# Input projections of a hybrid decoder block on one Trainium2 core: direct products, and seven products of quarters (Strassen) in two halves of the tokens

## Chip, cores and metric

The kernel runs on one core of one Trainium2 chip. The metric is the device time of one execution in microseconds (us). The kernel before was timed in three runs; the figure that stands for it is their median. The span of the profile is a profiled execution of its own.

## The reference

One decoder block over 2048 tokens of width 1024. The change lies in the first product, `xn @ w_in`, whose 6152 columns are q, k and v (1024 each), 8 forget logits, an attention gate, the input of a linear recurrent unit and its gate (1024 each):

```python
def rmsnorm(x, g):
    y = xf * lax.rsqrt(jnp.mean(xf * xf, axis=-1, keepdims=True) + RMS_EPS) * g
...
xn = rmsnorm(h, pre_gain[i])
z = xn @ w_in[i]
q, k, v, fl, g_attn, x_lru, g_lru = jnp.split(z, SPLIT_POINTS, axis=-1)
fl = fl + b_f[i]
o_attn = forgetting_attention(q, k, v, fl)          # 8 heads of 128, causal, scale 128 ** -0.5
y_attn = rmsnorm(o_attn, attn_out_gain[i]) * jax.nn.silu(g_attn)
xc = causal_depthwise_conv(x_lru, conv_w[i], conv_b[i])       # 4 taps
o_lru = rg_lru(xc, ...)       # two 128x128 gates per block of channels, then a scan over the tokens
y_lru = rmsnorm(o_lru, lru_out_gain[i]) * jax.nn.silu(g_lru)
mix = jnp.concatenate([y_attn, y_lru], axis=-1) @ w_out[i]
...
```

After it come a norm, the per-layer input embeddings and a sigmoid gate of another 1024x1024 product. All values are float32.

## The kernel before

**Products in three parts.** A float32 operand is split into a high part in TensorE's reduced format (fp32r) and a low part: `split` (L44) lets ScalarE round the high part (L46) and VectorE or GpSimd subtract it from the source (L52). `mm3` (L55) multiplies high by high, high by low and low by high (L60 to L62), so a product of two operands takes three matmuls, all added up in PSUM.

**Operands.** The tokens come transposed from memory (`xT`), the columns of a chunk being 512 tokens. Four chunks of x times the gain of the norm are split into `xh` and `xl` (L224 to L234), 8 pieces of 128 channels in each; they stay in SBUF to the end of the projections. The scale of each token's norm is computed beside it: ScalarE squares rows of x (L243), `rsqrt_small` takes the root, and a product with a diagonal matrix spreads the scales over the partitions (`rx`, L253). It is applied only when a result leaves PSUM.

**Value projection.** `load_wv` loads and splits weights of two heads (256 columns, 264 with the forget logits), `project_v` (L188) multiplies them with 16 blocks of 128 tokens as the stationary operand. The first two of the four groups are mixed with the loading of the chunks.

**The other projections** run over the eight head blocks `hb`. For each, `load_w` (L309) loads and splits 128 columns of weights, and `project` (L319) makes one bank of PSUM for a chunk: 8 pieces times 3 matmuls of 512 columns. In this order: x_lru for all chunks (L357 to L370), the convolution on VectorE (L367), the gate g_lru (L376 to L382), k, and between k's chunks the two gates of the recurrent unit (12 matmuls for each 512 tokens) with their chain: sigmoids, tanh and square root on ScalarE, reciprocal, two products, a scan and the gated output on VectorE (L401 to L413), the product with XC, the square and the sum of squares on GpSimd (L405, L420, L421). Then q and the attention gate of the head block before (L427). `spill` (L324) scales the result and stores it to memory. GpSimd also makes the low parts of most weights and of XC.

**What sets the order.** Each engine works off its own queue in the order in which a planner lays the program; tiles of the pools (`bank` 6, `wf` 2, `wh` 2 and so on) tie the queues to one another. All loads and stores of this stage are issued by SyncE (SP), in order. Attention (all of head 0's keys and values are loaded and split during the last projections, `load_part`, L432), the output product and the last gate follow; the change leaves their code, apart from the engine that splits keys and values (GpSimd becomes VectorE) and the place of the query's scale.

Of the kernel before, what the change touches and what calls it, by code (L numbers as in the profile page):

```python
# [65 lines left out]
def hymba_kernel(ctx: ExitStack, tc: tile.TileContext, x, xT, pT, w_t, w_v3, w_v4, w_o, w_ple, w_pg,  # L66
# [96 lines left out]
    def load_wv(pool, j):  # L163

        n = 264 if j == 3 else 256
        src = w_v4 if j == 3 else w_v3[j]
        wh = pool.tile([P, KD, 264], F32R, name="wvh")
        wl = pool.tile([P, KD, 264], F32R, name="wvl")
        yield wh, wl
        for q in range(4):  # L170
# [4 lines left out]
            yield

    def all_wv(pool, j):
        steps = load_wv(pool, j)
        w = next(steps)
        for _ in steps:  # L180
            pass
        return w

    def project_v(w, j, t2s=range(8)):
        n = 264 if j == 3 else 256
        wh, wl = w
        for t2 in t2s:
            vo = pva.tile([P, 2, 256], F32, name="vo", bufs=2)  # L188
            for ti in range(2):
                tb = t2 * 2 + ti  # L190
                ts = slice(tb % 4 * P, (tb % 4 + 1) * P)
                b = bank()
                for k in range(KD):
                    mm3(nc, b[:, :n], (xh[tb // 4][:, k, ts], xl[tb // 4][:, k, ts]), (wh[:, k, :n], wl[:, k, :n]),
                        k == 0, k == KD - 1)
                nc.scalar.activation(vo[:, ti], b[:, :256], AF.Copy, scale=rs_x[:, tb:tb + 1])
                if j == 3:
                    nc.vector.tensor_scalar(zf[:, :, tb], b[:, 256:264], rs_x[:, tb:tb + 1], None, ALU.mult)
# [4 lines left out]
    with ExitStack() as pv:  # L203
# [919 lines left out]
```

## Time and profile before

| | us |
|---|---|
| median of 3 runs | 2305.82 |
| lowest, highest run | 2304.03, 2310.03 |
| span of the profiled execution | 2304.8 |
| first matmul | 5.7 |
| end of the projections | 1139 |

| stage (profiled execution) | us |
|---|---|
| value projection and loading of x | 0 to 200 |
| the eight head blocks and the last two weights | 200 to 1139 |
| attention, output product, last gate | 1139 to 2304.8 |

How to read it: the page gives each engine's busy time, its share of the span and its instructions. PE is TensorE's matmuls, PEld its weight loads (beside the matmuls), DVE is VectorE, ACT ScalarE, POOL GpSimd, SP SyncE. A row of a group names the line, the engine, the operation, output and input tiles with their shapes, the count, then the busy time, the mean duration in ns, and the idle time of the engine ahead of the group with what ended it. A row of the timeline has the start, the duration, the engine, the line and the tiles. Matmuls overlap one another, so the duration of one is longer than the distance of two.

### The profile page before, as it was taken

The numbers are of one execution on the slowest core, as the hardware profiler recorded it, in microseconds if no ns is written. First come the engines' busy times: TensorE is split into PE (matmuls) and PEld (weight loads), VectorE is DVE, ScalarE is ACT, GpSimd is POOL, SyncE is SP. The second block draws the span as 40 slices with busy tenths as digits, with TensorE's granted clock in tenths as the row PEclk, the third lists the DMA queues.
The fourth block names the chain that finished last, engine by engine and source line by source line (L and its number), as shares of the span: only waits on it lengthen the run. The fifth ranks groups of instructions, "written<-read, shape, count | busy, mean of one in ns | idle before, by whom it ended". The sixth has DMA issues, their size and how long they took to land.

```text
span 2304.8 us, 30692 instructions
## 1 busy us (share of the span) xinstructions
PE 2271.1 (99%) x11425; PEld 1888.1 (82%) x11425; DVE 1205.8 (52%) x2190; ACT 929.2 (40%) x1558; POOL 668.5 (29%) x597
## 2 busy tenths in 40 slices
PE   8999999999999999999999999999999999999999
PEld 8998888888888888888788888888878887888887
DVE  5222675454546454546388888888833213333333
ACT  7312433332323232323267677776744323221111
POOL 0130323232323232313123344333544223222221
PEclk9999999999999999999999999999999999999999
DMA  9411112121212120212445444444446436333332
GB/s 339 138 51 37 53 48 78 37 85 37 85 37 85 37 85 32 81 35 79 130 124 158 147 157 144 134 123 139 157 123 203 153 126 201 131 104 119 107 108 75
DMA packets 169014, 249.02 MB, mean 108 GB/s; under 512 B 14241, under 2 KB 87201, under 8 KB 168865
## 3 DMA queue, kind: packets, MB, share of 16 engines
q1 hardware_dynamic: 168720, 247.03, 33.8%
q8 instruction: 89, 1.46, 0.3%
q14 instruction: 61, 0.49, 0.1%
q10 hardware_dynamic: 144, 0.05, 0.0%
HBM read 171.26 MB, written 75.76 MB: 107 GB/s over the span
## 4 chain that ended last, share of the span: by engine, by line
PE 93%; ACT 2%; DVE 2%; DMA 2%; issue 1%; SPq 0%; POOL 0%; ACTq 0%; DVEq 0%
PE bank L60 24%; PE bank L62 24%; PE bank L61 24%; PE tbank L665 5%; PE sbank L60 3%; PE obank L61 2%; PE obank L62 2%; PE sbank L61 2%; PE sbank L62 2%; PE obank L60 2%; ACT pr L638 1%; DMA kvf<-kT_d 1%; PE ebank L60 1%; PE ebank L61 1%; PE ebank L62 1%; PE tbank L684 1%
## 5 line engine op out<-in xcount | busy, mean ns | idle before, releaser
L60 PE MATMUL bank<-xh,wh 128*128 128x512 f32 x1280 | 506.0, 395 | 0.0
L61 PE MATMUL bank<-xl,wh 128*128 128x512 f32 x1280 | 505.9, 395 | 0.0
L62 PE MATMUL bank<-xh,wl 128*128 128x512 f32 x1280 | 505.9, 395 | 0.0
L61 PEld LDWEIGHTS bank<-xl,wh 128*128 128x128 f32 x1280 | 240.5, 188 | 58.0
L62 PEld LDWEIGHTS bank<-xh,wl 128*128 128x128 f32 x1280 | 240.5, 188 | 58.0
L60 PEld LDWEIGHTS bank<-xh,wh 128*128 128x128 f32 x1280 | 240.5, 188 | 57.8
L52 DVE TENSOR_TENSOR tl<-tbank,th 128x512 fp32r<-128x512 f32 (+1 forms) x320 | 192.8, 608 | 86.1 <-ACT th L46 82.2
L46 ACT ACTIVATE th<-tbank 128x512 fp32r<-128x512 f32 (+1 forms) x320 | 169.4, 532 | 132.4 <-PE tbank L665 129.7
L52 POOL TENSOR_TENSOR wl<-wf,wh 128x512 fp32r<-128x512 f32 x70 | 96.1, 1394 | 265.0 <-ACT wh L46 265.0
L665 PE MATMUL tbank<-ident,pr 128*128 128x128 f32 x1088 | 172.2, 274 | 0.0
L638 ACT ACTIVATE pr<-pr,m 128x128 f32<-128x128 f32 (+15 forms) x128 | 154.3, 1205 | 40.1 <-DVE m L629 38.9
L665 PEld LDWEIGHTS tbank<-ident,pr 128*128 128x128 f32 x1088 | 134.4, 141 | 29.2 <-issue 0.2
L60 PE MATMUL sbank<-kh,qh 128*128 128x512 f32 (+3 forms) x320 | 137.6, 430 | 15.2 <-DVE m L629 13.0
L60 PE MATMUL bank<-wvh,xh 128*128 128x256 f32 (+1 forms) x512 | 144.0, 285 | 7.2 <-ACT wvh L46 7.2
L52 POOL TENSOR_TENSOR yo<-yf,yh 128x1024 fp32r<-128x1024 f32 x32 | 76.9, 2403 | 255.8 <-ACT yh L46 255.7
L62 PE MATMUL bank<-wvh,xl 128*128 128x256 f32 (+1 forms) x512 | 144.5, 284 | 0.0
L61 PE MATMUL bank<-wvl,xh 128*128 128x256 f32 (+1 forms) x512 | 144.1, 283 | 0.0
L60 PE MATMUL obank<-th,vh 128*128 128x512 f32 (+1 forms) x320 | 123.7, 387 | 0.8 <-ACT th L46 0.8
L61 PE MATMUL obank<-tl,vh 128*128 128x512 f32 (+1 forms) x320 | 118.4, 370 | 1.2 <-DVE tl L52 0.6
L61 PE MATMUL sbank<-kl,qh 128*128 128x512 f32 (+3 forms) x320 | 117.5, 367 | 0.0
L62 PE MATMUL obank<-th,vl 128*128 128x512 f32 (+1 forms) x320 | 117.4, 367 | 0.0
L62 PE MATMUL sbank<-kh,ql 128*128 128x512 f32 (+3 forms) x320 | 117.0, 366 | 0.0
(218 smaller groups left out, 4589.1 us busy)
## 6 DMA issues: line engine op xcount, KB each, us to landing
wf<-in_w_t_dram SPq DMA_DIRECT2D x80, 256.0 KB, 3.0
xr<-in_x_dram SPq DMA_DIRECT2D x16, 512.0 KB, 6.5
v_d<-vo SPq DMA_DIRECT2D x64, 128.0 KB, 2.1
kT_d<-st SPq DMA_DIRECT2D x32, 256.0 KB, 2.1
yl_d<-G SPq DMA_DIRECT2D x32, 256.0 KB, 2.1
qT_d<-st SPq DMA_DIRECT2D x32, 256.0 KB, 2.1
gT_d<-st SPq DMA_DIRECT2D x32, 256.0 KB, 2.1
dg<-nb_d SPq DMA_DIRECT2D x32, 256.0 KB, 7.1
```

Source lines behind the costliest of these rows:

```text
L46: nc.scalar.activation(hi, src, AF.Copy)
L52: eng.tensor_tensor(out=lo, in0=src, in1=f32(hi), op=ALU.subtract)
L60: nc.tensor.matmul(out, lhsT=wh, rhs=xh, start=start, stop=False)
L61: nc.tensor.matmul(out, lhsT=wh, rhs=xl, start=False, stop=False)
L62: nc.tensor.matmul(out, lhsT=wl, rhs=xh, start=False, stop=stop)
L638: nc.scalar.activation(pr[0][:, :L], pr[0][:, :L], AF.Exp, bias=m2, scale=-1.0, accum_out=u.r4[:, i:i + 1])
L665: nc.tensor.transpose(b[:, i * P:(i + 1) * P], u.P[i][:, sb * P:(sb + 1) * P], ident)
L684: nc.tensor.transpose(b[:, i * P:(i + 1) * P], u.r4[:, i:i + 1].broadcast_to([P, P]), ident)
```

## The change

**Quarters.** Two projections of the same tokens are paired: k and q of a head, two heads of the attention gate, x_lru and g_lru of a block, two times 258 columns of v with two forget logits each. The weights (1024 channels by two column groups) and the tokens (1024 channels by two chunks of 512) are each cut in two by two, and Strassen's algorithm in Winograd's form needs seven products of quarters instead of eight. Each product has 4 pieces times 3 matmuls.

**Tokens.** The scale of the norm is now multiplied into the tokens before the split (`normalize`), and the seven token operands `XH[i]`, `XL[i]` (four of them differences, on GpSimd) hold one half of 1024 tokens. So the projections run in two passes, over tokens 0 to 1023 and 1024 to 2047, and load every weight twice.

**Weights.** A `Unit` is one pair in one pass. `prepare` makes a product's weight operand: a sum or difference on GpSimd for products 1 to 4, the high part `oh` on ScalarE, the low part `ol` on GpSimd for products 0, 2 and 5 and on VectorE for the others. `operand` keeps five of them prepared ahead of the product that is being multiplied. Four units (`light`, the attention gate in the second pass) use VectorE in place of GpSimd.

**Results.** `pair` copies products 0 and 1 out of PSUM by ScalarE, and puts the others together by six adds on VectorE, each with one PSUM input, and one add on GpSimd. The gates of a recurrent unit are put off: they are issued inside the next unit, behind its fifth product. They and the convolution now take 1024 tokens at a time, in tiles twice as wide.

The weights are packed as quarters on the host. The core of the diff, with the new functions:

```diff
+    XH = [xp.tile([P, 4, 512], F32R, name=f"XH{i}") for i in range(7)]
+    XL = [xp.tile([P, 4, 512], F32R, name=f"XL{i}") for i in range(7)]
...
+        def prepare(self, i):
...
+                if i == 1:
+                    src = wp.tile([P, WS], F32, name="ws", bufs=2)[:, :n]
+                    self.S.append(src)
+                    light.tensor_tensor(out=src, in0=a21, in1=a22, op=ALU.add)
+                elif i in (2, 3):
+                    src = self.S[hf]
+                    a, b = (src, a11) if i == 2 else (a12, src)
+                    light.tensor_tensor(out=src, in0=a, in1=b, op=ALU.subtract)
+                elif i == 4:
+                    src = a21
+                    light.tensor_tensor(out=src, in0=a11, in1=a21, op=ALU.subtract)
+                else:
+                    src = {0: a11, 5: a12, 6: a22}[i]
+                hi = wp.tile([P, WS], F32R, name="oh", bufs=NOP)
+                lo = wp.tile([P, WS], F32R, name="ol", bufs=NOP)
+                split(nc, src, hi[:, :n], lo[:, :n], "act", "pool" if i in (0, 2, 5) and not self.light else "dve")
...
+    mids = [("l", 0), ("k", 0), ("g", 0), ("l", 1), ("k", 1), ("l", 2), ("k", 2), ("g", 1), ("l", 3), ("k", 3),
+            ("l", 4), ("k", 4), ("g", 2), ("l", 5), ("k", 5), ("l", 6), ("k", 6), ("l", 7), ("k", 7), ("g", 3)]
+    mids_B = [(k, n) for n in range(6) for k in "lk"] + [("l", 6), ("l", 7), ("k", 6), ("k", 7)]
...
+    units_A = [unit("v", 0, 0)] + [unit(k, n, 0) for k, n in mids] + [unit("v", 1, 0)]
+    last_g = [("g", 0), ("g", 1), ("g", 2), ("g", 3)]
+    units_B = ([unit("v", 0, 1)] + [unit(k, n, 1) for k, n in mids_B] + [unit("v", 1, 1)]
+               + [unit(k, n, 1) for k, n in last_g])
+    for u in units_B[-4:]:
+        u.light = True
...
+    def multiply(u, i):
+        b = bank()
+        (wh, wl), = operand(u, i)
+        for k in range(4):
+            ks = slice(k * P, (k + 1) * P)
+            mm3(nc, b, (wh[:, ks], wl[:, ks]), (XH[i][:, k], XL[i][:, k]), k == 0, k == 3)
+        return b
...
+    def pair(u, done, into=lambda n, t: t):
...
+        nc.scalar.activation(t5, multiply(u, 1), AF.Copy)
+        add(t2, multiply(u, 2), t1)
+        (nc.vector if u.light else nc.gpsimd).tensor_tensor(out=t5, in0=t2, in1=t5, op=ALU.add)
+        b = multiply(u, 3)
...
+        add(o, b, t5)
+        done(0, 1, o)
+        b = multiply(u, 4)
+        add(t5, b, t5)
+        add(t2, b, t2)
+        done(1, 1, t5)
+        for f in pending[:1]:
+            pending.pop(0)()
...
+    with ExitStack() as s0:
...
+        for n in range(2):
+            row_scales(sg, 0, n)
+            for kh in range(2):
+                s[n, kh] = stage_tile(sg, 0, n, kh)
+            r = spread_scales(sg, 0, n)
+            for kh in range(2):
+                normalize(s[n, kh], r, kh)
...
+        for i in (1, 2, 3, 4, 6):
+            fill_operand(i, s)
+        kq_early(early)
+        v_unit(units_A[0], vp)
...
+    run_pass(0, units_A[1:-1])
...
+        s = load_stage(sg, 1)
+        v_unit(units_A[-1], vp, lambda i: fill_operand(i, s))
+        v_unit(units_B[0], vp)
+    run_pass(1, units_B[1:-5])
```

Where instructions move, two places. The first is SyncE's queue at the start of the program. `xf` and `s_...` are transposed tokens, `xr` and `c` rows of x for the norm's scales, `wvf` and `wf` weights. Before:

```order
L224 DMA xf<-in_xT_dram 128x2x256
L173 DMA wvf<-in_w_v_dram 128x528
L224 DMA xf<-in_xT_dram 128x2x256
L173 DMA wvf<-in_w_v_dram 128x528
L224 DMA xf<-in_xT_dram 128x2x256
L173 DMA wvf<-in_w_v_dram 128x528
L224 DMA xf<-in_xT_dram 128x2x256
L243 DMA xr<-in_x_dram 128x1024 x2
L173 DMA wvf<-in_w_v_dram 128x528
```

and now:

```order
L463 DMA c<-in_x_dram 128x512 x8
L472 DMA s_159<-in_xT_dram 128x1024 x2
L472 DMA s_162<-in_xT_dram 128x1024 x2
L463 DMA c<-in_x_dram 128x512 x7
L472 DMA s_234<-in_xT_dram 128x1024 x2
L472 DMA s_237<-in_xT_dram 128x1024 x2
L190 DMA wf<-in_w_p_dram 128x512 x4
L188 DMA wf<-in_w_v_dram 128x516 x3
```

The first weights stood second in the queue and alternated with pieces of 256 tokens; now the rows and the transposed tokens of the first 1024 tokens, all but one half row, stand ahead of them.

The same place on VectorE, as it is now. `s00` and `s01` are the first 512 tokens, `s10` and `s11` the second, `c`, `o11` and `u1` results of the first products, `ol` low parts of weights:

```order
L489 SCALAR_TENSOR_TENSOR s00_159<-s00_159,vec_70,rx_178 128x512 x4
L489 SCALAR_TENSOR_TENSOR s01_162<-s01_162,vec_70,rx_178 128x512 x4
L56 TENSOR_TENSOR XL0_109<-s00_159,XH0_102 128x512 x4
L56 TENSOR_TENSOR XL5_114<-s01_162,XH5_107 128x512 x4
...
L56 TENSOR_TENSOR ol_478<-ws_475,oh_477 128x516
L483 COPY rx_253<-sbank_240 128x512
L278 TENSOR_TENSOR o11_411<-bank_481,u1_409 128x258
L489 SCALAR_TENSOR_TENSOR s10_234<-s10_234,vec_70,rx_253 128x512 x4
L489 SCALAR_TENSOR_TENSOR s11_237<-s11_237,vec_70,rx_253 128x512 x4
```

The normalization of the second 512 tokens stands behind an add that reads a bank of v's second product.

The second place is the steady state, on GpSimd. Before, in a head block (`wl`, `XL`: low parts of weights and of XC; `I`, `R`, `accl`: steps of the recurrent unit):

```order
L52 TENSOR_TENSOR wl<-wf,wh 128x512 x4
L405 TENSOR_TENSOR I<-I,XC 128x512
L52 TENSOR_TENSOR XL<-XC,XH 128x512 x2
L405 TENSOR_TENSOR I<-I,XC 128x512
L420 TENSOR_TENSOR R<-R 128x512
L421 TENSOR_TENSOR accl<-accl,R 128x512
L52 TENSOR_TENSOR XL<-XC,XH 128x512
L52 TENSOR_TENSOR wl<-wf,wh 128x512 x2
```

and now in a pair of units of the second pass (`ws` and `wf` as outputs: sums and differences of weight quarters, `ol` low parts of weights, `c` the add of a product, `xcl` the low part of XC):

```order
L211 TENSOR_TENSOR ws_6476<-wf_6366,wf_6368 128x512
L292 TENSOR_TENSOR c_6240<-c_6239,c_6240 128x512
L218 TENSOR_TENSOR wf_6366<-wf_6364,wf_6366 128x512
L449 TENSOR_TENSOR R_6145<-R_6145 128x1024
L215 TENSOR_TENSOR ws_6317<-ws_6317,wf_6208 128x512
L450 TENSOR_TENSOR accl_5513<-accl_5513,R_6145 128x1024
L56 TENSOR_TENSOR ol_6342<-ws_6317,oh_6341 128x512
L215 TENSOR_TENSOR ws_6317<-wf_6214,ws_6317 128x512
L56 TENSOR_TENSOR ol_6420<-wf_6214,oh_6419 128x512
L56 TENSOR_TENSOR xcl_6393<-XC_6387,xch_6392 128x1024
```

Between the sum `ws_6476` of one product and the low parts of others now lie the add of a product and two steps of the recurrent unit of 1024 columns each.

More of the change, by code (lines that the diff above doesn't have):

```diff
@@ L177, in all_wv @@
[L177 to L198, printed above, removed]
-            for hh in range(2):
-                nc.sync.dma_start(out=v_d[2 * j + hh, :, t2 * 2:t2 * 2 + 2, :],
-                                  in_=vo[:, :, hh * P:(hh + 1) * P])
@@ new lines, in hymba_kernel, with operand @@
+    state = {"next": 0, "held": 0}
+    def operand(u, i):
+        while state["next"] < len(queue):
+            w, j = queue[state["next"]]
+            if state["held"] + w.halves > NOP:
+                break
+            w.prepare(j)
+            state["held"] += w.halves
+            state["next"] += 1
+            if j == 3:
+                nxt = [x for x, _ in queue[state["next"]:] if x is not w][:1]
+                if nxt and nxt[0].raw is None:
+                    nxt[0].load_all()
+        state["held"] -= u.halves
+        return u.ready.pop(i)
@@ new lines, in run_pass @@
+    def run_pass(p, us, extra=()):
+        with ExitStack() as q:
+            lw = pool_(q, f"lw{p}", side="right")
+            accl = lw.tile([P, NT], F32, name="accl", bufs=1)
+            if p == 0:
+                lam = lw.tile([P, NH], F32, name="lam", bufs=1)
+                lmx = lw.tile([P, NH], F32, name="lmx", bufs=1)
+                nc.vector.tensor_copy(lam, vec[:, LAM:LAM + NH])
+                nc.vector.tensor_scalar(lmx, lam, -1.0, 0.0, ALU.mult, ALU.max)
+                for _ in log1p_exp_neg_abs(sp4, lam, lw, NH):
+                    pass
+                nc.vector.tensor_tensor(out=sp4, in0=sp4, in1=lmx, op=ALU.add)
+                nc.vector.tensor_scalar(sp4, sp4, 4.0, None, ALU.mult)
+            for a, u in enumerate(us):
+                run(u, lw, accl)
+                if p == 0 and a in (3, 9):
+                    row_scales(lw, 1, a // 9)
+            while pending:
+                pending.pop(0)()
@@ L509, in load_u, with scaled_split @@
             u.dg.append((L - n, dg))
+    def scaled_split(q, hi, lo):
+        nc.scalar.activation(hi, q, AF.Copy, scale=QSCALE)
+        nc.vector.scalar_tensor_tensor(out=lo, in0=q, scalar=QSCALE, in1=f32(hi), op0=ALU.mult, op1=ALU.subtract)
     def split_u(u):
```

579 lines of the change are left out of this document (327 added, 252 removed).

## The prediction, made before the changed kernel was run

> **What bounds the kernel now.** I read the busy time first, then the stages, then what TensorE (PE) waits for.
>
> ```profile
> span 2304.8 us, 30692 instructions
> PE 2271.1 (99%) x11425; PEld 1888.1 (82%) x11425; DVE 1205.8 (52%) x2190; ACT 929.2 (40%) x1558; POOL 668.5 (29%) x597
> ```
>
> PE is busy 99%; VectorE (DVE) and GpSimd (POOL) are not near their limit. The windows (us, then each engine's busy time and count, clock, DMA share, GB/s) split the projections:
>
> ```profile
> 0.00:6.00 6.00, 0.29 (x1) 0.29 (x2) 1.54 (x4) 2.99 (x5) 1.33 (x11) 1.00 0.65 201
> 6.00:14.00 8.00, 6.53 (x37) 6.07 (x37) 5.31 (x14) 5.60 (x11) 0.46 (x1) 1.00 1.02 366
> 14.00:50.00 36.00, 36.00 (x301) 35.90 (x301) 22.06 (x49) 31.43 (x60) 1.97 (x3) 1.00 1.04 390
> ...
> 100.00:200.00 100.00, 100.00 (x836) 99.49 (x835) 16.57 (x67) 19.38 (x40) 24.92 (x9) 1.00 0.22 60
> ```
>
> ```profile
> 200.00:1139.00 939.00, 939.00 (x4037) 756.64 (x4035) 505.77 (x642) 305.61 (x414) 264.00 (x207) 1.00 0.19 61
> ```
>
> From 14 us to 1139 us PE never stops: 939/4037 = 0.2326 us for a matmul of 512 columns, 100/836 = 0.1196 us for one of 256. DVE works 54% and POOL 28% of the second window. So a matmul less is time less, as long as the other engines keep up. PE's waits, over the whole run:
>
> ```profile
> PE sbank L60 <- DVE m L629: 13.0, 19, 3.3
> PE bank L60 <- ACT wvh L46: 7.2, 2, 5.7
> ```
>
> Only the second lies in the projections: 5.7 + 1.5 = 7.2 us at the start.
>
> **What goes.** The 40 projections of 128 columns take 40 x 4 x 8 x 3 = 3840 matmuls of 512; seven products instead of eight make 3360. 480 x 0.2326 = 111.6 us. The value projection goes from 1536 to 1344 matmuls: 192 x 0.1196 = 23.0 us, less 1344 x 0.1196 x 2/256 = 1.3 for 258 columns. Sum **133.3 us**. The gate matmuls (192) and all that follows the projections stay; attention's query split costs DVE a scalar_tensor_tensor for a tensor_tensor, hidden as before. Weights are now read in both passes: 20 MB more over 1000 us, 20 GB/s on top of 61.
>
> **What it adds.** Every weight operand is now made (sum, high part, low part) in both passes and every product is put together outside PSUM. Prices:
>
> ```profile
> L402 DVE RECIPROCAL Dn<-Dn 128x512 f32<-128x512 f32 x32 | 107.3, 3353 | 1.1
> ...
> L52 POOL TENSOR_TENSOR yo<-yf,yh 128x1024 fp32r<-128x1024 f32 x32 | 76.9, 2403 | 255.8 <-ACT yh L46 255.7
> ...
> L46 ACT ACTIVATE wh<-wf 128x512 fp32r<-128x512 f32 x80 | 46.3, 625 | 100.2 <-PE bank L61 93.5 <-DMA wf<-in_w_t_dram 6.7
> ...
> L405 POOL TENSOR_TENSOR I<-I,XC 128x512 f32<-128x512 f32 x32 | 41.4, 1293 | 149.5 <-ACT I L399 149.5
> ...
> L420 POOL TENSOR_TENSOR R<-R 128x512 f32<-128x512 f32 x28 | 29.2, 1043 | 64.0 <-DVE G L413 64.0
> ...
> L331 DVE SCALAR_TENSOR_TENSOR st<-bank,vec,st 128x512 f32<-128x512 f32 x32 | 24.0, 749 | 15.9 <-ACT st L330 15.8
> ...
> L380 DVE TENSOR_TENSOR bank<-bank,rx 128x512 f32<-128x512 f32 x32 | 22.4, 699 | 79.7 <-PE bank L62 79.7
> ...
> L1013 DVE TENSOR_TENSOR xt<-mt,xt 128x1024 f32<-128x1024 f32 x15 | 18.4, 1225 | 0.5
> ...
> L409 DVE TENSOR_TENSOR_SCAN R<-Dn,I 128x512 f32<-128x512 f32 x8 | 9.8, 1224 | 0.3
> ...
> L52 DVE TENSOR_TENSOR wl<-wf,wh 128x512 fp32r<-128x512 f32 x10 | 6.6, 687 | 8.9 <-ACT wh L46 8.9
> ```
>
> The other gate steps of DVE, undisturbed, from the timeline:
>
> ```profile
> 680.61 0.68 DVE L406 TENSOR_TENSOR X<-X,Dn 128x512 f32<-128x512 f32 x1
> 681.39 0.69 DVE L407 TENSOR_TENSOR I<-I,X 128x512 f32<-128x512 f32 x1
> 682.00 0.42 DVE L408 TENSOR_SCALAR Dn<-Dn 128x512 f32<-128x512 f32 x1
> ```
>
> A k unit: PE 84 x 0.2326 = 19.5 us; POOL eight instructions (four sums, three low parts, the add of t5) x 1.29 = 10.3; DVE six adds x 0.70 + four low parts x 0.69 = 7.0. An l unit has 12 gate matmuls more (22.3 us). POOL adds three instructions of 1024 x 2.40, R squared 2 x 1.04 and wgl (about 1.2): 20.8. DVE has the same 7.0, the convolution 6 x 0.78 = 4.7 (below), the reciprocal 6.7, the scan 2.4, and X, I, Dn twice, both G steps in halves (2 x 0.68 + 2 x 0.69 + 4 x 0.42 + 2 x 0.75 + 2 x 0.69 = 7.3): 28.1. A g unit: PE 19.5, POOL 10.3, DVE 7.0 + 4 x 0.75 = 10.0. ACT gets 18 conversions x 0.63 = 11.3 a pair on top of the 14 it has now (34% of the second window): 25 of 42, hidden. An l and a k unit need PE 41.9, DVE 35, POOL 31: PE is longest, if the three run side by side. They don't. POOL's pair of splits alone and with a convolution beside it, then DVE's convolution alone, beside that pair, and beside another:
>
> ```profile
> 667.93 2.55 POOL L52 TENSOR_TENSOR wl<-wf,wh 128x512 fp32r<-128x512 f32 x2 [19.30 <-ACT wh L46]
> ```
>
> ```profile
> 294.65 3.44 POOL L52 TENSOR_TENSOR wl<-wf,wh 128x512 fp32r<-128x512 f32 x2
> ```
>
> ```profile
> 640.99 2.33 DVE L367 SCALAR_TENSOR_TENSOR XC<-X,vec,XC 128x512 f32<-128x512 f32 x3 [0.69 <-ACT XC L363]
> ...
> 646.72 3.25 DVE L367 SCALAR_TENSOR_TENSOR XC<-X,vec,XC 128x512 f32<-128x512 f32 x3 [1.02 <-ACT XC L363]
> ```
>
> ```profile
> 295.17 4.26 DVE L367 SCALAR_TENSOR_TENSOR XC<-X,vec,XC 128x512 f32<-128x512 f32 x3
> ```
>
> Both lose: 2.55 becomes 3.44 (1.72 for each split) and 2.33 becomes 4.26. A DVE instruction that reads PSUM loses nothing beside POOL, here 0.75 beside 1.30, their usual times:
>
> ```profile
> 614.84 0.75 DVE L331 SCALAR_TENSOR_TENSOR st<-bank,vec,st 128x512 f32<-128x512 f32 x1 [0.67 <-ACT st L330]
> ```
>
> ```profile
> 614.83 1.30 POOL L421 TENSOR_TENSOR accl<-accl,R 128x512 f32<-128x512 f32 x1
> ```
>
> Where the two take turns, one of each costs about 1.73 us, where alone they take 1.27 + 0.75 = 2.02: a share of 0.86. Of DVE's time these SBUF instructions are 2.8 in a k unit, 5.8 in a g unit and 2.8 + 4.7 + 2.4 + 7.3 = 17.2 in an l unit. An l and a k unit then hold POOL and DVE one after the other for 31.1 + 20.0 = 51.1 us of durations, or 44.0 at 0.86, where PE needs 41.9: short by at least 2.1 us a pair. The upper value comes from the queue: between the sum for a k unit's third product and its low part, POOL has operations of other steps (add, difference, R squared, ws, accl, then ol: 4 x 1.29 + 2.1 + 2.4 = 9.7) and takes turns with about 7 us of DVE's gate steps, 16.7 in all; five operands ahead give four products, 11.2. Late by 5.5. I take the middle, 3.8 us a pair: the convolution's two rows lie on both sides of it. Of 16 pairs four are followed by a g unit (16.1 x 0.86 = 13.8 of 19.5 us), which takes up the gates: 12 x 3.8 = 46. Where l6 and l7 stand side by side in the second pass, DVE has 28 us in l7's 22.3: 8 with its turns. **Passes: 54 us** (25 to 120).
>
> By the Trainium skill ("SBUF — State Buffer", section "SBUF: two separate sides") GpSimd and a VectorE instruction with two SBUF inputs lock a shared port pair, exclusively, for the whole instruction. The trace agrees that both wait (4.26 for 2.33). It speaks against this change, and with whole durations it gives the first rival.
>
> **Start.** PE's first matmul was at 5.7 us. Now SyncE queues 15 half-rows of x and 4.2 MB of xT (8.1 MB) ahead of the first weights, which end at 8.4 MB. By the windows 0.201 x 6 + 0.366 x 8 = 4.1 MB have moved by 14 us, then 390 GB/s: 25 us, and PE starts at 26. Four early products and two of v (11.2 + 11.5) end at 51, with 2 us for the slow matmuls of a start (37 in 6.53 us, 0.176 each). DVE normalizes the second 512 tokens only behind the first add of v's second product (46): 8 x 0.75, four splits of 1024 at 1.22, in turn with POOL's differences at 2.4, to about 66; the third product ends at 72. The fourth needs the next differences (4.8), their high and low parts: from 75, and four products of 5.7 end at 98. PE's work in it is 51.4, so 46.6 are lost, against 7.2 and 2: **37 us** (25 without turns taken, 50).
>
> **Between the passes and at the end.** While v's two units run (2 x 40.2 us of PE), POOL has for the first of them differences 8 x 2.40, weights 14 x 1.29 and t5 in four halves: 40 us; DVE on SBUF 16 x 0.75 + 14 x 1.22 + 8 x 0.69 = 35. The second has 21 and 6. At 0.86 of 102 = 88 this meets 80.4 and 6 us of g3's slack, but the first unit carries 64 of it in 40: **12 us** (0 to 25). The last four g units make operands on DVE: 18 x 0.69 + 4 x 0.75 = 15.4 of 19.5 us; head 0's eleven splits bring two of them to 38.5 of 39: **3 us** (0 to 10). The forget gates' pow steps (eight, 23.3 us in all) lie under the first two.
>
> **Sum.** 2304.8 - 133.3 + 54 + 37 + 12 + 3 = 2277.5; the median of the runs is 2305.82, 1.0 above the profiled span: **2278.5 us**.
>
> **Rivals.**
> 1. Slower: POOL and DVE on SBUF, not PE, set the passes. Each instruction keeps the other out for its whole duration: 51.1 us a pair, 9.2 over PE; 12 x 9.2 + 8 = 118 instead of 54, and 2342. For it: 4.26 us for 2.33, and POOL's queue above; against: DVE waits for PE in part of every unit, where POOL runs free. It decides from 81 us, 6 us a pair.
> 2. Much faster: collisions fall into DVE's own waits, and operands five products ahead cover them: 10 us instead of 54, and 2234. For it: the sums at 0.86 exceed PE by 2.1 us a pair only; against: that asks both queues to be full without a gap.
> 3. The losses cancel the gain, within 0.3% (6.9 us, about what a measurement of this kernel can tell from no change): 2299 to 2313, with passes at 74 to 88 us.
>
> The forecast's case gets 0.37, rival 2 0.14, rival 3 0.13, rival 1 0.36. Faster 0.51, same 0.13, slower 0.36. The range of 8 in 10 leaves the ends of rivals 1 and 2: 2230 to 2348; the forecast's own, with its start and middle terms, 2250 to 2299.
>
> **What would show it.** PE at 3552 matmuls of 512 and 1344 of 258 with the same cadence; first matmul near 26 us and l0 near 98; PE waiting on low parts (ol) from POOL and DVE, some 4 us in each pair not followed by g; DVE's convolution and POOL's splits longer than 0.75 and 1.29. If PE's waits in a pass stay under 10 us, rival 2 holds; if POOL or DVE never idles in the second pass and PE waits over 6 us a pair, rival 1. A first matmul before 20 us, or a value projection at another cadence, would make the start or the saving wrong.

## The result, and the profile after

The changed kernel takes 2383.95 us (median of 4 runs, 2382.17 to 2385.34), the kernel before 2305.41 (4 runs, 2304.03 to 2310.03): a ratio of 1.0337, with a 95% interval of 1.0322 to 1.0352. The forecast was 2278.5 us, with a range of 2230 to 2348. It is slower, and by more than the worst of the rivals (2342) gave.

Units are called by what they project: v the values, l the recurrent unit's input with its gate, k the keys with the queries, g two heads of the attention gate; l0 is the l unit of block 0. `xch` and `xcl` are the high and low part of XC, the convolved input that the two gates are computed from. The page of the changed kernel, its span and the engines' busy time:

```profile
span 2381.2 us, 30652 instructions
PE 2200.0 (92%) x10753; PEld 1807.6 (76%) x10753; DVE 1612.8 (68%) x2363; ACT 1039.8 (44%) x1786; POOL 1172.8 (49%) x865
```

PE was busy for 99% of the span and is so for 92%. The windows of the changed kernel by stage: up to the first product, the start with v, the first pass, the two v units between the passes, the second pass, its last v unit, the last four g units, and the rest of the kernel. Columns as before (length, then busy time and count of PE, PEld, DVE, ACT, POOL, then the granted clock, DMA share, GB/s):

```profile
0.00:27.10 27.10, 3.18 (x8) 2.00 (x8) 10.39 (x20) 16.24 (x41) 2.34 (x12) 1.00 0.94 351
27.10:111.50 84.40, 62.55 (x391) 57.48 (x392) 64.81 (x63) 27.21 (x43) 67.93 (x42) 0.84 0.27 78
111.50:572.60 461.10, 422.47 (x1732) 332.80 (x1731) 376.71 (x356) 202.65 (x323) 320.73 (x194) 0.96 0.28 90
572.60:686.80 114.20, 94.68 (x697) 91.40 (x696) 100.70 (x117) 37.88 (x61) 88.10 (x57) 0.91 0.37 120
686.80:1080.00 393.20, 354.03 (x1443) 276.82 (x1443) 320.38 (x256) 167.08 (x249) 267.58 (x165) 0.96 0.24 75
1080.00:1128.70 48.70, 43.40 (x344) 42.74 (x343) 34.87 (x52) 11.01 (x22) 26.80 (x21) 0.96 0.38 114
1128.70:1214.20 85.50, 80.99 (x349) 65.69 (x348) 64.13 (x123) 35.07 (x59) 26.18 (x13) 0.96 0.38 113
1214.20:2381.20 1167.00, 1138.66 (x5802) 938.67 (x5800) 640.85 (x1379) 542.67 (x991) 373.12 (x365) 0.99 0.45 137
```

The projections end at 1214.2 us where they ended at 1139; what follows takes 1167.0 us, 1.2 more than before. So the whole difference lies in the projections. To see where, I take from each window what its matmuls need at full pace (0.2326 us for 512 columns, and 0.1196 x 258 / 256 = 0.1205 for 258) and call the rest lost:

| stage | length | matmuls need | lost | of it by the clock | forecast of the loss |
|---|---|---|---|---|---|
| to l0's first product | 111.5 | 48 x 0.2326 + 336 x 0.1205 = 51.7 | 59.8 | 13.5 | 46.6 |
| first pass | 461.1 | 1728 x 0.2326 = 401.9 | 59.2 | 18.4 | 54 for both passes |
| two v units between | 114.2 | 672 x 0.1205 = 81.0 | 33.2 | 10.3 | 12 |
| second pass | 393.2 | 1440 x 0.2326 = 334.9 | 58.3 | 15.7 | (above) |
| last v unit | 48.7 | 40.5 | 8.2 | 1.9 | 0 |
| last four g units | 85.5 | 336 x 0.2326 = 78.2 | 7.3 | 3.4 | 3 |
| sum | 1214.2 | 988.2 | 226.0 | 63.2 | 115.6 |

"By the clock" is one minus the granted clock of the window's row, times its length: an upper value, since a part of the half-clock time fell on an idle PE. The kernel before has 1139 us, of which its matmuls need 4032 x 0.2326 + 185.1 = 1122.9 (185.1 for v, 1152 of 256 columns and 384 of 264), so it lost 16.1. The account: 1122.9 - 988.2 = 134.7 us saved, 226.0 - 16.1 = 209.9 lost, 1.2 more behind: 76.4, the difference of the two spans.

What PE waited for in the changed kernel up to 1225 us, some of the longest sums (us in total, times, longest):

```profile
PE bank L66 <- DVE ol L56: 24.4, 15, 2.9
PE bank L64 <- ACT oh L50: 22.6, 14, 9.2
PE bank L64 <- ACT xch L50: 18.5, 4, 6.7
...
PE bank L66 <- DVE XL L56: 12.3, 4, 4.9
PE bank L64 <- ACT XH L50: 11.9, 3, 8.6
PE bank L64 <- DVE c L278: 11.4, 8, 2.3
PE bank L66 <- POOL ol L56: 11.0, 12, 1.8
```

No single tile: low parts, high parts, XC's parts for the gates, banks that an add should have emptied. The trace also shows where they lie, when the passes are cut at the first product of each unit. In the second pass the first seven l units take 19.4 to 19.6 us for their 84 matmuls, which is full pace. All of its loss is in the eight units that follow an l unit, in which that block's gates are issued (k0 to k5, l7, k6): 27.0 to 31.1 us for 96 matmuls that need 22.3. In the first pass the four g units run at full pace too, but the k units ahead of them (k0, k2, k4, k7) lose 4.3 to 9.5 us each, and l1, l3 and l5 right behind a g unit lose 4.6, 3.5 and 1.4. As an example l4 and k4 of the second pass, then k4, g2 and l5 of the first:

```profile
880.40:899.90 19.50, 19.50 (x86) 15.79 (x85) 19.46 (x12) 4.56 (x9) 11.15 (x8) 1.00 0.21 68
899.90:931.00 31.10, 25.17 (x98) 18.68 (x97) 23.73 (x24) 16.00 (x23) 24.67 (x16) 0.95 0.26 89
360.00:391.70 31.70, 26.13 (x97) 19.43 (x96) 23.00 (x25) 16.23 (x24) 25.48 (x17) 0.89 0.25 87
391.70:411.20 19.50, 19.50 (x86) 15.77 (x85) 19.46 (x15) 6.53 (x11) 11.76 (x7) 1.00 0.18 56
411.20:432.10 20.90, 19.81 (x85) 15.53 (x84) 18.55 (x19) 8.00 (x14) 17.51 (x12) 1.00 0.35 126
```

(A window also counts the matmuls that overlap its edges.) The waits don't make up the loss: by the windows by stage PE is idle for 152.9 of the 1214.2 us, and 226.0 are lost. Three windows from the longest wait of the second pass on (6.7 us for `xch`) show the rest:

```profile
1043.80:1050.50 6.70, 0.24 (x2) 0.00 (x0) 6.70 (x7) 0.92 (x1) 4.30 (x2) 0.77 0.13 39
1050.50:1053.90 3.40, 3.21 (x8) 2.53 (x9) 3.40 (x3) 0.77 (x2) 3.37 (x2) 0.50 0.55 155
1053.90:1057.30 3.40, 3.40 (x16) 2.76 (x15) 2.88 (x3) 0.00 (x0) 3.40 (x3) 0.95 0.33 124
```

After the idle stretch PE has work again, but for 3.4 us the granted clock is 0.50 and 8 matmuls pass, where 16 do in the next 3.4 us at 0.95. That was not in the forecast.

VectorE and GpSimd in the second pass of the changed kernel, groups of instructions with their mean:

```profile
L405 DVE TENSOR_TENSOR G<-c,G 128x512 f32<-128x512 f32 x16 | 28.8, 1818 | 5.8 <-ACT G L404 5.8
...
L440 DVE TENSOR_TENSOR_SCAN R<-Dn,carry,I 128x1024 f32<-128x1024 f32 x7 | 21.4, 3058 | 0.2
...
L399 DVE COPY X<-halo 128x3 f32<-128x3 f32 x8 | 14.5, 1818 | 0.0
```

```profile
L292 POOL TENSOR_TENSOR c<-c 128x512 f32<-128x512 f32 x16 | 28.7, 1794 | 3.5 <-DVE c L278 3.5
L218 POOL TENSOR_TENSOR wf<-wf 128x512 f32<-128x512 f32 (+1 forms) x15 | 25.5, 1701 | 0.2
```

In these two groups GpSimd's 1.29 has become 1.7 to 1.8; VectorE's product with G takes 1.82 where 0.69 was its price, and a copy of three columns takes 1.82. One of these copies, with the GpSimd instruction beside it:

```profile
930.12 2.37 DVE L399 COPY X<-halo 128x3 f32<-128x3 f32 x1
```

```profile
929.61 2.86 POOL L436 TENSOR_TENSOR I<-I,XC 128x1024 f32<-128x1024 f32 x1
```

The copy ends at 932.49 and the GpSimd instruction at 932.47: what the copy takes is the rest of the other's time. Neither engine is full: of 393.2 us VectorE is busy 320.4 and GpSimd 267.6.

### The profile page after: what moved, and what is told of

It is laid out like the page before. It is cut to its first block, busy times and chain, and to the rows that moved or that the text cites. A ratio compares the mean times of both kernels' runs of the same rounds, so it can differ in the third digit from the quotient of the medians.

```text
span 2381.2 us, 30652 instructions
## 1 busy us (share of the span) xinstructions
PE 2200.0 (92%) x10753; PEld 1807.6 (76%) x10753; DVE 1612.8 (68%) x2363; ACT 1039.8 (44%) x1786; POOL 1172.8 (49%) x865
## 5 line engine op out<-in xcount | busy, mean ns | idle before, releaser
L64 PE MATMUL bank<-XH,oh 128*128 128x512 f32 x1120 | 454.5, 406 | 35.4 <-ACT oh L50 22.4
L66 PE MATMUL bank<-XH,ol 128*128 128x512 f32 x1120 | 450.5, 407 | 35.4 <-DVE ol L56 24.4
L65 PE MATMUL bank<-XL,oh 128*128 128x512 f32 x1120 | 451.0, 403 | 0.0
L66 PEld LDWEIGHTS bank<-XH,ol 128*128 128x128 f32 x1120 | 216.8, 194 | 98.6 <-DVE ol L56 31.8
L64 PEld LDWEIGHTS bank<-XH,oh 128*128 128x128 f32 x1120 | 217.2, 194 | 94.8 <-ACT oh L50 30.4
L65 PEld LDWEIGHTS bank<-XL,oh 128*128 128x128 f32 x1120 | 217.1, 194 | 50.5
L50 ACT ACTIVATE oh<-ws 128x512 fp32r<-128x512 f32 (+1 forms) x144 | 90.6, 629 | 267.6 <-POOL ws L215 130.9
L56 POOL TENSOR_TENSOR ol<-wf,oh 128x512 fp32r<-128x512 f32 (+1 forms) x88 | 129.2, 1471 | 134.7 <-ACT oh L50 120.0
L278 DVE TENSOR_TENSOR c<-bank,c 128x512 f32<-128x512 f32 x208 | 137.9, 680 | 70.9 <-POOL c L292 35.3
L845 PEld LDWEIGHTS tbank<-ident,pr 128*128 128x128 f32 x1088 | 134.7, 141 | 29.4 <-issue 0.4
L64 PE MATMUL bank<-oh,XH 128*128 128x258 f32 x448 | 133.1, 302 | 24.8 <-ACT XH L50 11.9
L66 PE MATMUL bank<-oh,XL 128*128 128x258 f32 x448 | 129.7, 298 | 12.3 <-DVE XL L56 12.3
L65 PE MATMUL bank<-ol,XH 128*128 128x258 f32 x448 | 133.3, 300 | 5.7 <-DVE ol L56 3.9
```

Of the source, the lines that this page charges most:

```text
L50: nc.scalar.activation(hi, src, AF.Copy)
L56: eng.tensor_tensor(out=lo, in0=src, in1=f32(hi), op=ALU.subtract)
L64: nc.tensor.matmul(out, lhsT=wh, rhs=xh, start=start, stop=False)
L65: nc.tensor.matmul(out, lhsT=wh, rhs=xl, start=False, stop=False)
L66: nc.tensor.matmul(out, lhsT=wl, rhs=xh, start=False, stop=stop)
L278: nc.vector.tensor_tensor(out=o, in0=x, in1=y, op=ALU.add)
```

## The experiments

Theories: **A**, the lock: GpSimd's and VectorE's instructions on SBUF shut one another out, and their summed durations set the passes (the forecast's ground, and rival 1's). **B**: VectorE's whole queue time sets them, with or without the lock. **C**: the hand-over of t5 from GpSimd to VectorE inside a unit. Others came up on the way. Unless said otherwise a kernel is the changed one (2383.95 us) with the edit shown, timed once with a profile, and "the passes lose" is the length of its two passes less the 736.9 us that their matmuls need; in the changed kernel it is 117.4.

**Leaving out the reciprocal.**

```diff
-            nc.vector.tensor_scalar(Dn, R, 1.0, None, ALU.add)
-            nc.vector.reciprocal(Dn, Dn)
+            nc.vector.tensor_scalar(Dn, R, -0.5, 1.0, ALU.mult, ALU.add)
```

> The recurrent unit's reciprocal is left out (its input is formed as 1 - R/2, one VectorE instruction as before), so 16 x 6.54 = 105 us go from VectorE's queue, of an instruction that no GpSimd instruction lengthens. Theory A, the lock (GpSimd's instructions and VectorE's on SBUF shut one another out, and their summed durations set the passes): little, 2360 to 2384 us. Theory B, VectorE is full (its queue's whole time sets the passes): 2285 to 2320 us. Theory C, the hand-over (VectorE's adds wait for GpSimd's add of t5): 2355 to 2384 us.

2340.45 us. Its two passes:

```profile
110.80:564.20 453.40, 419.25 (x1740) 330.16 (x1739) 313.08 (x350) 202.86 (x324) 307.66 (x195) 0.97 0.29 93
671.00:1043.50 372.50, 344.05 (x1443) 273.43 (x1442) 261.07 (x252) 167.57 (x248) 266.24 (x163) 0.97 0.25 80
```

They lose 453.4 + 372.5 - 736.9 = 89.0. That is between the theories: 105 us of VectorE that no GpSimd instruction touches gave 43, so the lock isn't all (A fails here), and VectorE's time isn't all (B wanted at least 64). C's range (2355 to 2384) is missed too.

**Leaving out the convolution's taps and the products with Q.**

```diff
-        for j in (2, 1, 0):
+        for j in ():
             nc.vector.scalar_tensor_tensor(out=XC, ...
...
-            nc.vector.tensor_tensor(out=Q, in0=Q, in1=Dn, op=ALU.mult)
-            nc.vector.tensor_tensor(out=I, in0=I, in1=Q, op=ALU.mult)
```

> The convolution's three taps on VectorE and the two products with Q are left out (XC is only scaled): by their durations in the changed kernel's profile 48 x 1.76 + 16 x (1.69 + 1.92) = 142 us of VectorE, about 100 us of it without the time in which GpSimd shuts them out; all of it on SBUF. Theory A (lock): clearly more than leaving out the reciprocal, 2285 to 2325 us, and GpSimd's instructions shorter. Theory B (VectorE is full): 2285 to 2320 us, about the same as without the reciprocal. Theory C (hand-over): 2350 to 2384 us.

2310.44 us:

```profile
113.70:538.80 425.10, 408.36 (x1732) 326.79 (x1731) 304.96 (x321) 203.52 (x326) 308.37 (x195) 0.99 0.31 99
651.20:1014.30 363.10, 342.09 (x1443) 272.44 (x1442) 260.18 (x223) 167.45 (x248) 268.99 (x165) 0.99 0.26 85
```

The passes lose 51.3. As much VectorE time as the reciprocal when undisturbed (100 against 105 us), but on SBUF, and it gains 73.5 against 43.5. That would give A and B a part each, but the two edits differ in more than the lock: the convolution stands ahead of `xch`, and with it gone PE no longer waits for `xch` at all, where it had waited 18.5 us. How much of the 30 us between them is lock and how much is this shorter chain stays open. GpSimd's busy time hardly fell (308 and 269 us, from 321 and 268), against A's second sign.

**Leaving out the square and its sum on GpSimd.**

```diff
-            else:
-                nc.gpsimd.tensor_tensor(out=R, in0=R, in1=R, op=ALU.mult)
-                nc.gpsimd.tensor_tensor(out=accl, in0=accl, in1=R, op=ALU.add)
```

> The square of R and its sum on GpSimd are left out for head blocks 1 to 7: 14 x (2.0 + 2.4) = 62 us of GpSimd's queue, all on SBUF. Theory A (lock): 2325 to 2355 us. Theory B (VectorE is full): 2365 to 2384 us. Theory C (hand-over): 2350 to 2375 us, since these two stand ahead of operands and of the add of t5.

2366.66 us, 17 less for 62 us of GpSimd; the passes lose 110.5. That is short of A's 29 and inside the ranges of B (2365 to 2384) and C (2350 to 2375).

**Product 1 added from PSUM.**

```diff
-        nc.scalar.activation(t5, multiply(u, 1), AF.Copy)
-        add(t2, multiply(u, 2), t1)
-        (nc.vector if u.light else nc.gpsimd).tensor_tensor(out=t5, in0=t2, in1=t5, op=ALU.add)
+        p5 = multiply(u, 1)
+        add(t2, multiply(u, 2), t1)
+        add(t5, p5, t2)
```

> Product 1 stays in PSUM and VectorE adds it to t2 there: GpSimd loses 36 adds of 1.8 us (65 us), ScalarE 36 copies, VectorE gets 36 x 0.68 = 24 us more, of a form that GpSimd doesn't lengthen, and VectorE no longer waits for GpSimd inside a unit (24 us of such waits in the second pass). The gates, v and the last four units stay. Theory A (lock): 2320 to 2355 us. Theory B (VectorE is full): 2384 to 2400 us. Theory C (hand-over): 2290 to 2330 us.

2382.13 us: no gain, though VectorE no longer waits for GpSimd inside a unit. Theory C falls, and A's 29 to 64 didn't come either; B's range (2384 to 2400) is missed by 2 us.

**The gate chain in halves of 512 tokens.**

```diff
+            def chain(n):
+                cs = slice(n * 512, (n + 1) * 512)
+                nc.vector.tensor_scalar(Dn[:, cs], R[:, cs], 1.0, None, ALU.add)
+                nc.vector.reciprocal(Dn[:, cs], Dn[:, cs])
...
+            chain(0)
+            chain(1)
```

> The recurrent unit's chain on VectorE (sum, reciprocal, two products, scale, scan) and its GpSimd product run in two halves of 512 tokens, the same work in twice the instructions, so that an add or a low part waits for 3.3 us at most where it waited for 6.5. Theory A (lock) and theory B (VectorE is full): no gain, 2380 to 2395 us. Theory D, the lump (the gate chain stands as one block in VectorE's queue ahead of low parts and adds, and five operands ahead don't cover it): 2335 to 2365 us.

2421.07 us, 37 slower, and the passes lose 151.2. Theory D falls; more and shorter instructions on VectorE and GpSimd made it worse, which no theory had said.

**Operands on VectorE in all k, l and g units.**

```diff
-    for u in units_B[-4:]:
-        u.light = True
+    for u in units_A + units_B:
+        u.light = u.kind != "v"
```

> All k, l and g units make their operands and the add of t5 on VectorE, as the last four do: per l and k pair 16 instructions of 1.29 us leave GpSimd and come to VectorE with 0.69 us each. Theory A (lock): the durations that shut one another out fall from 51 to about 41 us a pair, 2300 to 2340 us. Theory B (VectorE is full): VectorE has 11 us more a pair and loses some 7 of waiting for GpSimd, 2384 to 2420 us. Theory D (lump): the low parts stand behind still more, 2390 to 2440 us.

2334.99 us: A's range. The passes, and the VectorE groups that were shown of the second one:

```profile
109.00:548.30 439.30, 414.02 (x1732) 327.80 (x1731) 408.79 (x505) 204.34 (x324) 97.78 (x46) 0.98 0.29 94
660.60:1030.60 370.00, 345.33 (x1444) 274.11 (x1443) 350.68 (x380) 168.28 (x248) 94.02 (x43) 0.97 0.25 80
```

```profile
L440 DVE TENSOR_TENSOR_SCAN R<-Dn,carry,I 128x1024 f32<-128x1024 f32 x7 | 16.4, 2342 | 0.0
...
L405 DVE TENSOR_TENSOR G<-c,G 128x512 f32<-128x512 f32 x16 | 10.3, 680 | 0.1
...
L399 DVE COPY X<-halo 128x3 f32<-128x3 f32 x8 | 1.3, 158 | 0.0
```

The passes lose 72.4. VectorE does 16 instructions more a pair and yet the same product with G falls from 1.82 to 0.68 us, the copy from 1.82 to 0.16, the scan from 3.06 to 2.34: that much of the changed kernel's VectorE time was waiting for GpSimd. VectorE is now busy 350.7 of 370 us: it is the next bound.

**All low parts of the units that aren't light on GpSimd.**

```diff
-split(nc, src, hi[:, :n], lo[:, :n], "act", "pool" if i in (0, 2, 5) and not self.light else "dve")
+split(nc, src, hi[:, :n], lo[:, :n], "act", "dve" if self.light else "pool")
```

> All low parts of weights of the units that aren't light are made on GpSimd: per pair 8 instructions of 0.69 us leave VectorE, 8 of 1.29 us come to GpSimd (31 + 10 = 41 us of 41.9 that PE needs). Theory A (lock): 56 us of durations a pair instead of 51, 2430 to 2470 us. Theory B (VectorE is full): 2350 to 2384 us. Theory D (lump): operands no longer stand behind the gate chain, 2330 to 2375 us, unless GpSimd itself is full by then.

2404.39 us; the passes lose 138.1. The second one:

```profile
701.60:1095.60 394.00, 357.40 (x1444) 281.42 (x1443) 277.58 (x194) 167.25 (x249) 370.37 (x229) 0.93 0.24 75
```

VectorE is relieved (277.6 us instead of 320.4) and the pass is no shorter, since GpSimd is busy 370 of 394. B falls. D had excepted the case that GpSimd is full, which this is, so nothing speaks for or against it here. A has the sign right, and gave 25 us too much.

**An exponential for the decay.**

```diff
-            nc.vector.tensor_scalar(Dn, R, 1.0, None, ALU.add)
-            nc.vector.reciprocal(Dn, Dn)
+            nc.scalar.activation(Dn, R, AF.Exp, scale=spn[:, hb:hb + 1])
...
-            nc.vector.tensor_tensor(out=Q, in0=Q, in1=Dn, op=ALU.mult)
+            nc.vector.scalar_tensor_tensor(out=Q, in0=Dn, scalar=1.0, in1=Q, op0=ALU.add, op1=ALU.mult)
...
-            nc.vector.tensor_scalar(Dn, Dn, 2.0, -1.0, ALU.mult, ALU.add)
```

> The decay comes from an exponential on ScalarE (16 instructions of 1.1 us and up to two table loads a unit) in place of sum, reciprocal and scale on VectorE, and (1 + decay) goes into the product with Q: the unit computes the same. VectorE loses 6.5 + 2 x 1.4 us a unit, 149 us in all with its waits, where leaving out the reciprocal took 105 and gained 43. Theory A (lock): 2335 to 2345 us. Theory B (VectorE is full) and theory D (lump): 2310 to 2335 us.

2366.27 us, 18 less than the changed kernel; the passes lose 115.4, against 89.0 without the reciprocal, though VectorE is freer still. None of the theories gave that. One thing that differs is ScalarE, which makes the high parts: it is busy 420 us in the two passes (370 there), with 28 table loads in the eight blocks of the second pass, where the changed kernel has 15. That these loads are the cause wasn't tested. In its second pass:

```profile
L432 ACT ACT_TABLE_LOAD x8 | 10.3, 1283 | 0.1
...
L435 ACT ACT_TABLE_LOAD x8 | 10.3, 1283 | 0.1
...
L405 ACT ACT_TABLE_LOAD x7 | 9.0, 1283 | 19.7 <-DMA yl_d<-G 19.6
...
L431 ACT ACT_TABLE_LOAD x5 | 6.4, 1283 | 0.1
```

**Gaps in the kernel before.** Its projections have next to no idle time (1.5 us from the first product on, in 1133.3), so the price of a gap can be read alone. Theory **E**: the clock is granted at half for some time after an idle stretch. **F**: the slow matmuls only wait for operands.

```diff
+    def hold(w, n):
+        for _ in range(n):
+            nc.scalar.activation(w[0], f32(w[0]), AF.Copy)
...
+                    if c:
+                        hold(w, 1)
                     b = project(w, c)
```

> The kernel before, with 48 gaps in TensorE's work: ahead of the second to fourth chunk of each x_lru and g_lru projection ScalarE copies the weights' high part onto itself once (1.1 us), after the last product has read it and before the next may. Each gap should be 1.3 to 1.7 us of idle TensorE, 62 to 82 us in all. Theory E, the clock (an idle stretch of TensorE over about 2 us is followed by 3.4 or 6.8 us at half the granted clock): no half-clock records from these gaps, 2368 to 2390 us. Theory F (the slow matmuls of the changed kernel come from waits for operands, not from the clock): the same.

2368.74 us (the kernel before beside it 2308.96). Its waits, then its granted clock:

```profile
PE bank L60 <- ACT wh L321: 50.1, 48, 2.5
```

```profile
core 0: 2366.9 us, clock 0.997
```

48 gaps of 1.04 us, 50.1 in all; the time rose by 59.8, 0.2 us a gap beyond the idle time, and the clock is what it is without gaps (0.997). The same with `hold(w, 2)`:

> The same with two copies: 48 gaps of 2.3 to 2.8 us, 110 to 135 us of idle. Theory E (clock): nearly every gap is followed by a record of half the granted clock and costs 1.7 to 3.4 us more than its idle time: 2500 to 2590 us. Theory F: the idle time alone, 2416 to 2440 us.

2502.3 us:

```profile
PE bank L60 <- ACT wh L321: 122.5, 48, 3.8
```

```profile
core 0: 2500.4 us, clock 0.970
```

48 gaps of 2.55 us on the average, 122.5 in all, and the time rose by 193.3: 70.8 us on top, 1.5 a gap. The granted clock fell by 0.027 of 2500 us, 67.5 us of lost pace, so about 135 us at half clock, 2.8 us for each gap. Theory E is shown: the time is in its range, the price of a gap a little under the 1.7 to 3.4 that it gave. F falls. In the changed kernel the clock is 0.969, by the same count 0.028 x 2381 = 67 us. Gaps between 1.04 and 2.55 us weren't tried.

**Six operands ahead.**

```diff
-NOP = 5
+NOP = 6
...
-        r = pool.tile([P, 512], F32, name="rx", bufs=2)
+        r = ctile()
```

> Six operands ahead instead of five (the scales rx take a tile of the ring c to make room); no work is added or removed. Theory G, the lead (operands pass through three queues in turn and come late now and then; more lead covers it): 2340 to 2365 us. Theory A (lock) and theory B (VectorE is full): the passes are set by summed work, 2375 to 2390 us.

2399.49 us, 15 slower; the passes lose 129.3. More lead is no cure (theory G falls), and it lies outside the range of A and B as well. That it costs is not explained: the planner lays the queues anew for each kernel, so a single edit that moves the time by less than some 30 us shows no mechanism by itself.

**Token differences on VectorE.**

```diff
-                nc.gpsimd.tensor_tensor(out=o, in0=a, in1=b, op=ALU.subtract)
+                nc.vector.tensor_tensor(out=o, in0=a, in1=b, op=ALU.subtract)
```

> The differences of the token operands (16 instructions of 1024 columns, 2.4 to 3.0 us each on GpSimd) go to VectorE at about 1.2 us. Only the start and the stage between the passes can change. Theory A (lock): the XL (2.3 us beside GpSimd, 1.2 alone) and the normalization (1.8 beside, 0.75 alone) get shorter, and of 60 and 34 us lost there 10 and 12 come back: 2355 to 2368 us. Theory B (VectorE is full there): 2380 to 2400 us.

2358.32 us, A's range. l0 begins at 98 instead of 111.5, and the stage between the passes takes 108.1 us instead of 114.2. The start:

```profile
25.90:98.00 72.10, 59.04 (x390) 55.22 (x391) 53.58 (x71) 27.68 (x43) 60.40 (x34) 0.88 0.32 98
```

VectorE does more instructions (71 for 63) in less time (53.6 for 64.8 us).

**Combinations.** The first puts operands and token differences on VectorE and adds product 1 from PSUM (three diffs above together).

> Three edits together: operands on VectorE in all k, l and g units (alone it gained 49 us), token differences on VectorE (alone 26 us), product 1 added from PSUM (alone 2 us; here it only frees ScalarE, since the add is VectorE's already). Theory B' (with the lock mostly gone VectorE is the bound of the passes, 95% busy there): the gains add up at most, 2305 to 2312 us. Theory H (ScalarE's queue makes the operands late): 2290 to 2303 us, by the 36 copies that it no longer has.

2314.81 us; the single gains (49.0, 25.6 and 1.8) would have made it 2307.6, and B' is missed by 3 us; the passes lose 70.2. Theory H's sign fails. The second has the exponential too:

> The same with the exponential on ScalarE in place of sum, reciprocal and scale on VectorE: 16 x 8.5 = 136 us less on VectorE, a table load or two and 1.15 us more on ScalarE for each unit. Theory B' (VectorE is the bound): the passes lose 15 to 30 us instead of 72 and the time is 2250 to 2275 us. Theory H (ScalarE's queue): 2290 to 2310 us, no better than without it.

2327.26 us, slower than without it, and the passes lose 95.2 with VectorE only 80% busy (311 of 387 us in the second). B' fails; H has the sign, and its range is missed by 17 us. PE's longest waits in its projections:

```profile
PE bank L64 <- DVE c L279: 40.7, 17, 3.6
PE bank L64 <- ACT xch L50: 16.4, 9, 3.0
```

PE waits for a bank of PSUM that an add of VectorE should have emptied: product 1 now holds one of six until t2 is there. (The first combination has this edit too, and this wait is 24.2 us there.) The third has XC's low part on VectorE as well:

```diff
-        split(nc, XC, xch, xcl, "act", "pool")
+        split(nc, XC, xch, xcl, "act", "dve")
```

> The same as the one before, and XC's low part on VectorE (16 instructions of 1.2 us, for which GpSimd takes 2.4 to 3.8). TensorE waited 19.5 us for it with operands on VectorE. Theory B': 2245 to 2270 us, 5 to 12 better than without it. If VectorE has no room for 16 x 1.2 us more: 2255 to 2285, no better.

2310.34 us; the passes lose 81.8. Better by 17, but far from the range. The last two take the hand-overs away that PE now waited for: seven banks, and the gates issued behind a unit's last product instead of its fifth, with the exponential (d1) and with the reciprocal (d2). Both were timed four times.

```diff
-        return ps.tile([P, 512], F32, name="bank", bufs=6)
+        return ps.tile([P, 512], F32, name="bank", bufs=7)
...
-        return ps.tile([P, 512], F32, name="sbank", bufs=2)
+        return ps.tile([P, 512], F32, name="sbank", bufs=1)
...
-        for f in pending[:1]:
-            pending.pop(0)()
         if not u.early:
...
         done(1, 0, t2)
+        for f in pending[:1]:
+            pending.pop(0)()
```

> The last combination (operands, token differences and XC's low part on VectorE, product 1 from PSUM, the exponential), with seven banks instead of six and the gates two products later. If the hand-overs were what was left: the passes lose 20 to 35 us instead of 82, 2250 to 2270 us. If VectorE's own time is the bound: 2295 to 2310 us.

> The same without the exponential, so with the reciprocal's 6.5 us a unit on VectorE. If the hand-overs were what was left: 2265 to 2290 us, since VectorE (95% busy) then binds a little. If VectorE's own time was the bound all along: 2300 to 2315 us, as without the seven banks.

d1 takes 2291.76 us (4 runs, 2289.83 to 2292.92) against 2306.06 (7 runs) of the kernel before: a ratio of 0.994, interval 0.9923 to 0.9956. It is the one version that is faster, by 0.6%. It lies between the two ranges, and its passes lose 49.8 where 20 to 35 were expected:

```profile
96.80:521.20 424.40, 409.93 (x1732) 328.22 (x1731) 337.47 (x492) 214.33 (x321) 66.72 (x37) 0.98 0.30 98
627.60:989.90 362.30, 344.26 (x1444) 273.91 (x1443) 281.68 (x363) 185.83 (x255) 63.58 (x34) 0.98 0.25 81
```

The third combination (c3) lost 81.8 there, with the same work on every engine: the hand-overs were worth 32 us in the passes, of which 13 were lost again outside them (2310.34 to 2291.76 is 18.6). d1 still loses 45 at the start and 25 between the passes. d2 takes 2319.93 us, ratio 1.0061 (1.0046 to 1.0076): above both of its ranges, and no better than the first combination (c1). So the exponential, which gained 18 us alone and cost 12 between the first combination and the second, gains 28 between d2 and d1. These two pairs differ in the banks, the place of the gates and the engine of XC's low part, so which of the three turned the sign isn't shown.

The same two edits alone on the changed kernel:

> The changed kernel with seven banks of PSUM instead of six and the gates two products later; no work moves to another engine. Theory A (lock: the summed durations of GpSimd and VectorE set the passes): TensorE only waits elsewhere, 2370 to 2390 us. Theory C' (hand-over: the waits for banks and for XC's parts, 33 us of idle and some 12 of half clock, go away): 2335 to 2355 us.

2412.21 us, 28 slower; the passes lose 126.6 and the stage between them 44.8. PE waits elsewhere: for VectorE's low parts 40.4 us where it was 24.4. Theory C' falls: with GpSimd's work where the change put it, hand-overs weren't the bound. A's words fit (TensorE only waits elsewhere), its range (2370 to 2390) doesn't.

## Why the prediction was wrong

**The saving was right**: 133.3 forecast, 134.7 by the counts and the pace, and what follows the projections changed by 1.2 us. At full clock the pace is as before: 36 matmuls between these two starts in the last units, 0.231 us each.

```profile
1205.25 0.39 PE L64 MATMUL bank<-XH,oh 128*128 128x512 f32 x1
...
1213.58 0.40 PE L64 MATMUL bank<-XH,oh 128*128 128x512 f32 x1
```

**The price of idle time was missing.** The forecast counted an idle microsecond as one, and only the start got 2 us for slow matmuls. By the windows up to 63 us of the 226 lost are half clock; the kernel before with two copies in each gap shows the mechanism by itself. By the Trainium skill ("TensorE: Matmul & The Clock Gate", section "What's actually happening") the clock is halved after an idle window of about 3.4 us and restored after a busy one. The length agrees with the 3.4 us at 0.50 above; but gaps of 2.55 us on the average, shorter than that window, were enough. Without this the kernel would have taken at least 2384 - 67 = 2317 us: still slower, so it isn't the whole of the miss.

**The step that failed is the passes' 54 us: 3.8 us a pair, in 12 pairs of 16.** The forecast spread the work of GpSimd and VectorE evenly over an l and a k unit, and let the g unit behind four of the pairs take up what was over. Cut by units, the g units took up nothing: these four pairs, which had nothing in the forecast, lost 39.3 us with the l unit behind each g. The other four of the first pass lost 20.5 for 15.2, and the second pass 58.3 for 38.4 (eight pairs, and 8 us for l6 and l7 side by side). The loss isn't spread over a pair either. It lies in the unit behind an l unit, 58.3 / 8 = 7.3 us each in the second pass, some 5 of it idle and up to 2 clock, while seven of the eight l units lose nothing. The idle part is near the upper of the two values that the forecast had (5.5, from GpSimd's queue), where it took the middle. In sum 117.4 for 54.

**Rival 1 had the price (118), its mechanism only half.** That GpSimd and VectorE cost one another time is shown: the same instructions on VectorE are 1.1 us (G) and 1.7 us (a three-column copy) shorter with GpSimd's operands gone, and moving work off GpSimd gained 49 us, moving work onto it cost 20. But rival 1's own sign, that one of the two never idles, isn't there (81% and 68% busy), and the reciprocal, which takes 6.54 us with and without GpSimd's operands beside it, gave 43 us back. What fits the waits is the chain from sum to high part to low part through three queues, each of which also holds the recurrent unit's steps, with GpSimd and VectorE lengthening one another in two of them. This is argued from the waits; no experiment shows it by itself. How much is contention and how much queue, single edits didn't separate, and why more lead, halves, and later gates each made it slower is open.

**Rival 2** (collisions hidden by five operands ahead) falls with the passes' 117.4, and rival 3 (no change, 2299 to 2313) with the time.

**The start** was right in its places: first product at 27.1 (26 forecast). PE's waits there, for the second 512 tokens' operands, are the ones that the forecast named:

```profile
63.22 0.58 PE L64 MATMUL bank<-oh,XH 128*128 128x258 f32 x1 [8.56 <-ACT XH L50]
...
71.69 0.58 PE L66 MATMUL bank<-oh,XL 128*128 128x258 f32 x1 [4.89 <-DVE XL L56]
```

59.8 lost for 46.6, and the difference is mostly the clock: up to 13.5 for 2. **Between the passes** 33.2 for 12, up to a third of it clock. That the differences on GpSimd and VectorE's work stood in one another's way is shown by moving them to VectorE: the start then lost 98.0 - 51.7 = 46.3 us and the stage between the passes 27.1. The last v unit (8.2) had no term at all, since I took it as hidden.

## What to carry to other kernels

A kernel whose TensorE is busy 99% has slack on the other engines only as long as their work doesn't meet: before work is put there in exchange for matmuls, add up what the two engines do on SBUF, and put it on the one that does it in less time (here VectorE, 0.69 against 1.29 us), even if its share looks high. Price a gap of TensorE at more than its length: gaps of 2.55 us cost 1.5 us more here, gaps of 1.04 us 0.2. Don't average the load of the helping engines over a group of products: look at the unit in which the extra steps run, since the lighter units beside it didn't make up for it here. After a bound is removed, look for the next one in the waits: the exponential cost 12 us in one combination and gained 28 in another.

## What the runs showed of the hardware

- Gaps of 1.04 us in TensorE's work left the granted clock at 0.997; gaps of 2.55 us on the average brought it to 0.970 and cost 1.5 us each beyond their length.
- A VectorE copy of 128x3 took 1.82 us on the average beside a busy GpSimd, 0.16 with GpSimd's operands moved away. One of them ended within 0.02 us of the GpSimd instruction that ran beside it.
- With an exponential between sigmoids, tanh and square root ScalarE made 28 table loads of 1.28 us in eight blocks, where it made 15 without.
